# Four small loads moved out of a layer kernel's start, one normalisation a tick later, weight splits after attention steps

## The chip, the cores and the metric

The kernel runs on one core of one Trainium2 chip. The metric is device time in microseconds (us) of one execution; several runs are made and their median is quoted. Five engines matter here: PE (TensorE, matrix products), DVE (VectorE), ACT (ScalarE), POOL (GpSimd) and SP (SyncE, which here only issues transfers). POOL issues transfers as well. PEld is the load of the stationary operand of a product, which overlaps PE.

## The reference

One decoder layer on 512 tokens of width 1024. The input x is RMS-normalised and goes through one wide input projection. Three token mixers read it: block-sparse attention with partial rotary positions (MoBA, 8 heads of 64), forgetting attention with a cumulative log-gate bias (FoX, 8 heads of 64), and attention into 256 memory tokens (4 heads of 128). Queries and keys are normalised per head. The three results are projected, gated by sigmoids, summed and projected again; a SwiGLU feed-forward network follows. Cut to what the change touches:

```
h   = rms_norm(x, g_mix)
q_m = partial_rope(rms_norm(split_heads(q_m), g_q_moba))     # k_m alike
log_f = log_sigmoid(f_logit + b_forget)
mkv = rms_norm(mem, g_mem) @ w_mem_kv
y_c = softmax(q_c mk^T * scale) mv                           # memory attention
out = x + merged @ w_out, then + SwiGLU(rms_norm(.))
```

## The kernel before, in words

Every float32 product is made of three products: each operand is split into a rounded high half and the remainder (PASSES at L35: high by high, high by low, low by high). A weight arrives from HBM as a piece of 512 KB (`load_next`, L170, issued on SP), ACT writes its high half (`w_hi`, L234) and DVE subtracts to get the low half (`w_lo`, L237). `split_next` (L208) does one such piece; the low half of a piece is queued in `w_lows` and is issued by the next call, or by `take` (L252), which hands a finished piece to the products. Some pieces are sums of others (`w_sum`, L222), for a fast matrix product with seven instead of eight block products (`unit`, L764).

The order of all instructions is written out by hand. PE's products go through `mm` (L307), which counts their nominal time and calls `tick` (L291) every 1250 ns. A tick issues, in this order: what `head` holds, one weight split, what is due (`later(n, fn)`: n ticks from now, L328), steps of the work that runs beside (`beside`, L325: memory attention at 0.6 steps a tick, and so on), and what `pend` holds. A tick fixes only the order on each engine; when an instruction runs is settled by the semaphores. Each engine runs its list in order, so one that waits holds up all behind it.

The start goes like this. SP issues the two halves of the memory tokens, then weight pieces and the four tiles of x in turn (L408 to L423). POOL issues eight loads of small gains (L424 to L430), then four more: the rotary table of 64 KB (L432), two rows of 16 gains sent to all 128 partitions (L434, L435) and the eight forget biases sent to all partitions (L437). PE turns the memory tokens and multiplies them into memory keys and values (`mem_groups`, L521), 12 products to a piece. Beside it, one step a tick: two empty steps, `small_gains` (L482, which ends in six POOL products that make the rotary factors `cg` and `sg`, L494 and L497), the squares of x's four tiles (`square_x`, L656, on ACT), one empty step, squares of the memory, and then PE's turning of x (`turn_x`, L672, L676), two blocks a tick.

x's normalisation goes in two halves, `rms_x(0)` and `rms_x(1)` (L667). Each is three stages in `rsqrt` (L350): the variance on DVE (`rv`, L366), an estimate on ACT (L370, L371) and a Newton step on DVE (L374 to L376), and then `scale_x` (L660): POOL scales tiles 0 and 1, DVE scales tiles 2 and 3 (L663).

Then come the query projection of memory attention (`head_chunk`, L908; its 96 products make some 16 ticks), the gate parts, and two seven-product units, with memory attention beside them (`mem_attention`, L914). A step of it has, for one unit u of eight, scores on PE (L922), the row minimum on DVE (L930, L931), the exponentials on ACT (L939), the reciprocal on DVE and the scaling on POOL at the next tick (L943, L946), and three steps later PE's turning of the probabilities (L957), split by ACT and DVE (`memph`, `mempl`), and the values product (L968, split into `yT`). PE's results go to five banks of PSUM with the tag "a" and three with "m", in turn.

Of the kernel before, what the change touches and what calls it, by code (L numbers as in the profile page):

```python
# [17 lines left out]
P = 128  # L18
# [4 lines left out]
D = 1024  # L23
# [14 lines left out]
def f32(ap):  # L38
    return ap.bitcast(F32)
# [3 lines left out]
def hybrid_layer(ctx, tc, rope, x, mem, g_mix, w_in, b_forget, g_q_moba, g_k_moba, g_q_fox,  # L43
                 g_k_fox, g_q_mem, g_k_mem, g_mem, w_mem_kv, w_br_moba, w_br_fox, w_br_mem,
                 w_out, g_ffn, w_gate, w_up, w_down, out):
    nc = tc.nc
# [9 lines left out]
    def slot(name, dt=F32):  # L56
        return U.tile([P, SLOT], dt, name=name, tag="u", bufs=NSLOT)
# [26 lines left out]
    def dsrc(t, offset, pattern):  # L84
        return bass.AP(tensor=t.tensor, offset=t.offset + offset, ap=pattern)
# [72 lines left out]
    raws, split, used = {}, {}, {}  # L158
    st = {"load": 0, "split": 0, "take": 0, "stage": 0}
# [8 lines left out]
    w_lows = deque()  # L168
# [22 lines left out]
    def add_now(i):  # L191
        fn = accs.pop(i, None)
        if fn is not None:
            fn()

    def load_due():
        while st["load"] < len(loads):
            i = loads[st["load"]]
            if due.get(i, i - RAW_AHEAD) > st["split"]:
                return  # L200
            load_next()

    def drop(i):
        used[i] = used.get(i, 0) - 1
        if used[i] < 0:
            raws.pop(i)

    def split_next(least=0):  # L208


        if w_lows:
            w_lows.popleft()()
        i = st["split"]
        if i >= len(pieces) or i >= st["take"] + max(pace["ahead"], least):
            return
        kind, src, nk, w = pieces[i]
        n = nk * w
        if kind == "sum" and i not in raws:
            for j in src:
                add_now(j)  # L220
            r = raws[i] = slot("w_sum")
            dve.tensor_tensor(r[:, :n], raws[src[0]][:, :n], raws[src[1]][:, :n], op=OP.add)  # L222
            for j in src:
                drop(j)
            return
        add_now(i)
        if i not in split:
            split[i] = slot("w_hi", F32R), slot("w_lo", F32R)
        r, (hi, lo) = raws[i], split[i]
        if i < HALVES:  # L230
            c = slice(st["stage"] * n // 2, (st["stage"] + 1) * n // 2)
        else:
            c = slice(0, n)
        act.activation(hi[:, c], r[:, c], AF.Copy)  # L234

        def low():
            dve.tensor_tensor(lo[:, c], r[:, c], f32(hi[:, c]), op=OP.subtract)  # L237
        if i < HALVES:
            pend.append(low)
            st["stage"] = 1 - st["stage"]  # L240
            if st["stage"]:
                return
            run_pend()
            drop(i)
        else:
            w_lows.append(low)
            drop(i)
        split[i] = tuple(t[:, :n].rearrange("p (k c) -> p k c", k=nk) for t in (hi, lo))
        st["split"] += 1
        load_due()  # L250
# [13 lines left out]

    side = deque()
    deferred = []
    pace = {"credit": 0.0, "ns": 0, "ahead": 2}
    QUANTUM = 1250

    pend = []  # L270
# [1 line left out]
    def run_pend():  # L272
        for fn in pend:
            fn()
        pend.clear()
# [4 lines left out]
    def run_head():  # L280
        for fn in head:
            fn()
        head.clear()

    def run_due():
        due = [d for d in deferred if d[0] <= 1]
        deferred[:] = [[d[0] - 1, d[1]] for d in deferred if d[0] > 1]
        for d in due:
            d[1]()

    def tick():  # L291


        run_head()
        if w_lows or st["split"] < st["take"] + pace["ahead"]:
            split_next()
        run_due()
        if side:
            pace["credit"] += side[0][0]
            while pace["credit"] >= 1 and side:  # L300
                pace["credit"] -= 1
                side.popleft()[1]()
        if not side:
            pace["credit"] = 0.0
        run_pend()

    def mm(ps, lhsT, rhs, n, start, stop):  # L307
        if pace["ns"] >= QUANTUM:
            pace["ns"] = 0
            tick()  # L310
        pe.matmul(ps, lhsT, rhs, start=start, stop=stop)  # L311
        pace["ns"] += n * 0.42
# [12 lines left out]
    def beside(steps, rate):  # L325
        side.extend((rate, fn) for fn in steps)

    def later(n, fn):  # L328
        deferred.append([n, fn])
# [20 lines left out]
    def rsqrt(ss, inv_n, w, delay=None, rows=None, nh=1, out=None):  # L350

        v, y0, a, r = (sm(i, 32, 4 if i == "rr" else 3) for i in ("rv", "ry", "ra", "rr"))
        v, y0, a = v[:, :w], y0[:, :w], a[:, :w]
        r = r[:, :w] if out is None else out

        def by_rows(o, i):
            o3, i3 = (q.rearrange("p (t h) -> p t h", h=nh) for q in (o, i))
            dve.tensor_tensor(o3, i3, rows[:, :, None].to_broadcast([P, w // nh, nh]), op=OP.mult)  # L360

        def variance():
            if rows is not None:
                by_rows(ss, ss)
                by_rows(ss, ss)
            dve.tensor_scalar(v, ss, inv_n, EPS, op0=OP.mult, op1=OP.add)  # L366

        def estimate():
            use_table("natural_log_exp_and_others")
            act.activation(a, v, AF.Ln)  # L370
            act.activation(y0, a, AF.Exp, scale=-0.5)  # L371

        def newton():
            dve.tensor_tensor(a, y0, y0, op=OP.mult)  # L374
            dve.scalar_tensor_tensor(a, a, -0.5, v, op0=OP.mult, op1=OP.mult)
            dve.scalar_tensor_tensor(r, a, 1.5, y0, op0=OP.add, op1=OP.mult)  # L376
            if rows is not None:
                by_rows(r, r)
        for n, stage in enumerate((variance, estimate, newton)):
            if delay is None:  # L380
                stage()
            elif delay + n == 0:
                pend.append(stage)
            else:
                later(delay + n, stage)
        return r
# [42 lines left out]
    nc.gpsimd.dma_start(grow[GQC:GQC + 1], g_q_mem)  # L429
    nc.gpsimd.dma_start(grow[GKC:GKC + 1], g_k_mem)  # L430
    rope_t = first[:, 256:384].rearrange("p (t c) -> p t c", t=NT)
    nc.gpsimd.dma_start(rope_t, rope)  # L432
    grot = first[:, 384:416].rearrange("p (j c) -> p j c", j=2)
    nc.gpsimd.dma_start(grot[:, 0], dsrc(g_q_moba, 0, [[0, P], [1, 16]]))  # L434
    nc.gpsimd.dma_start(grot[:, 1], dsrc(g_k_moba, 0, [[0, P], [1, 16]]))  # L435
    bfor = consts.tile([P, 8], F32, name="bfor")
    nc.gpsimd.dma_start(bfor, dsrc(b_forget, 0, [[0, P], [1, 8]]))  # L437

    mz = consts.tile([P, 512], F32, name="mz")
    pool.memset(mz, 0.0)  # L440
# [41 lines left out]
    def small_gains():  # L482
        tg = bank("a")
        pe.transpose(tg[:, :NG], grow, ident[:NG, :NG])
        dve.tensor_copy(gcol, tg[:, :NG])
        for a in (0, 64):
            dve.memset(gcol[a:a + 16, GQM:GQM + 1], 1.0)
            dve.memset(gcol[a:a + 16, GKM:GKM + 1], 1.0)
        dve.tensor_scalar(gcol[:, GQF:GQM + 1], gcol[:, GQF:GQM + 1], -(64.0 ** -0.5), None, op0=OP.mult)
        dve.tensor_scalar(gcol[:, GQC:GQC + 1], gcol[:, GQC:GQC + 1], -(128.0 ** -0.5), None, op0=OP.mult)  # L490
        dve.tensor_scalar(gneg, gcol, -1.0, None, op0=OP.mult)
        for j in range(2):
            g = grot[:, j:j + 1, :].to_broadcast([P, NT, 16])
            pool.tensor_tensor(cg[:, j], rope_t[:, :, 0:16], g, op=OP.mult)  # L494
            for a in (0, 8):
                g8 = grot[:, j:j + 1, 8 - a:16 - a].to_broadcast([P, NT, 8])
                pool.tensor_tensor(sg[:, j, :, a:a + 8], rope_t[:, :, 16 + a:24 + a], g8, op=OP.mult)  # L497
# [156 lines left out]
    ssx = sm("ssx", NT, 1)  # L654
# [5 lines left out]
    def scale_x(t):  # L660
        r = rsx[t // 2][:, t % 2:t % 2 + 1]
        e = pool if t < 2 else dve
        e.tensor_scalar(x_t[t][:, :D], x_t[t][:, :D], r, 1.0, op0=OP.mult, op1=OP.mult)  # L663

    rsx = {}

    def rms_x(half):  # L667
        rsx[half] = rsqrt(ssx[:, 2 * half:2 * half + 2], 1.0 / D, 2, 0)
        later(2, lambda: scale_x(2 * half))
        later(2, lambda: scale_x(2 * half + 1))  # L670

    def turn_x(k, delay=None):  # L672

# [209 lines left out]
    def last_square(t):  # L883
        square_x(t)
        rms_x(t // 2)
# [17 lines left out]
    pre = None  # L903
    sums_of_h(6)
    pace["ahead"] = 3
    rs_q = consts.tile([P, NT * 4], F32, name="rs_q")
    nrs_q = consts.tile([P, NT * 4], F32, name="nrs_q")
    head_chunk(NT, 128, [(GQC, QC, h, gcol) for h in range(4)], lag=4, rs=rs_q)  # L908
# [254 lines left out]
        branch_part(bi, Y, jc)  # L1163


    later(9, lambda: beside(mem_attention(), 0.6))
    for jc in (0, 1):
        gate_part(0, jc)
# [1 line left out]
    tok_unit((heads_of("rope", GKM, KM, 0), heads_of("rope", GQM, QM, 0, gneg)))  # L1170
    tok_unit((values_of(VM, (0, 1)), values_of(VM, (2, 3))))
    pace["ahead"] = 2
    later(5, lambda: beside(attention((0, 1), QM, KM, VM, YM, None), 0.8))
    for jc in (0, 1):
        branch_part(0, YC, jc)
# [627 lines left out]
```

## Time and profile before

| | |
|---|---|
| median of 3 runs | 854.36 us (853.95 to 854.64) |
| the profiled execution, its own time | 853.07 us |
| its span, first to last instruction | 851.3 us, granted TensorE clock 1.00 |
| PE busy | 838.0 us (98%) |
| DVE, ACT, POOL busy | 688.5, 476.8, 202.1 us |

The time of the profiled execution is 1.8 us more than its span, and 1.3 us less than the median of the runs. Busy time on PE overlaps from one product to the next, so a gap that the profile shows is shorter than what was lost: the distance between two starts tells it.

### The profile page before, as it was taken

The numbers are of one execution on the slowest core, as the hardware profiler recorded it, in microseconds if no ns is written. First come the engines' busy times: TensorE is split into PE (matmuls) and PEld (weight loads), VectorE is DVE, ScalarE is ACT, GpSimd is POOL, SyncE is SP. The second block draws the span as 40 slices with busy tenths as digits, with TensorE's granted clock in tenths as the row PEclk, the third lists the DMA queues.
The fourth block names the chain that finished last, engine by engine and source line by source line (L and its number), as shares of the span: only waits on it lengthen the run. The fifth ranks groups of instructions, "written<-read, shape, count | busy, mean of one in ns | idle before, by whom it ended". The sixth has DMA issues, their size and how long they took to land.

```text
span 851.3 us, 14399 instructions
## 1 busy us (share of the span) xinstructions
PE 838.0 (98%) x5348; PEld 757.9 (89%) x5348; DVE 688.5 (81%) x1183; ACT 476.8 (56%) x820; POOL 202.1 (24%) x286
## 2 busy tenths in 40 slices
PE   7999999999999999999999999999999999999998
PEld 5778899899888889888999889999999999988886
DVE  4888799779686768877778757899989898897985
ACT  5946666576765648757435546453344444474571
POOL 5110428331532023324102021423210321110210
PEclk9999999999999999999999999999999999999999
DMA  9922357336922532754849546989955997864992
GB/s 308 352 37 75 75 134 188 51 100 184 290 74 59 165 76 80 175 92 142 255 128 287 204 129 128 228 174 209 178 132 112 183 183 179 215 151 149 245 250 91
DMA packets 146757, 137.66 MB, mean 162 GB/s; under 512 B 6192, under 2 KB 123496, under 8 KB 146688
## 3 DMA queue, kind: packets, MB, share of 16 engines
q1 hardware_dynamic: 111200, 104.65, 40.6%
q0 software_dynamic: 34304, 29.99, 23.1%
q10 hardware_dynamic: 1184, 2.12, 0.8%
q8 instruction: 42, 0.69, 0.3%
q14 instruction: 27, 0.22, 0.1%
HBM read 124.13 MB, written 8.40 MB: 156 GB/s over the span
## 4 chain that ended last, share of the span: by engine, by line
PE 87%; DVE 7%; ACT 3%; DMA 2%; issue 1%; SPq 0%; DVEq 0%; ACTq 0%
PE ps_m L311 38%; PE ps_a L1473 15%; PE ps_m L1473 11%; PE ps_a L1626 9%; PE ps_a L311 3%; PE ps_a L1062 3%; PE ps_a L1000 2%; PE ps_m L1626 2%; PE ps_a L1051 2%; DMA x_t<-in_x_dram 2%; DVE w_lo L237 2%; PE ps_a L606 1%; ACT p_t L939 1%; ACT w_hi L234 1%; PE ps_a L968 0%
## 5 line engine op out<-in xcount | busy, mean ns | idle before, releaser
L311 PE MATMUL ps_m<-w_hi,hT 128*128 128x256 f32 (+2 forms) x464 | 120.3, 335 | 0.0
L237 DVE TENSOR_TENSOR w_lo<-w_raw,w_hi 128x1024 fp32r<-128x1024 f32 (+2 forms) x90 | 105.0, 1180 | 7.9 <-ACT w_hi L234 7.0
L1473 PE MATMUL ps_a<-xh,wl 128*128 128x256 f32 x352 | 99.8, 284 | 0.1
L1473 PE MATMUL ps_a<-xh,wh 128*128 128x256 f32 x352 | 99.7, 283 | 0.0
L1473 PE MATMUL ps_a<-xl,wh 128*128 128x256 f32 x352 | 99.6, 283 | 0.0
L311 PE MATMUL ps_m<-hT,w_hi 128*128 128x512 f32 (+1 forms) x352 | 99.4, 369 | 0.0
L234 ACT ACTIVATE w_hi<-w_raw 128x1024 fp32r<-128x1024 f32 (+2 forms) x90 | 88.0, 1004 | 2.7 <-DMA w_raw<-in_w_in_dram 1.3
L311 PEld LDWEIGHTS ps_m<-w_hi,hT 128*128 128x128 f32 x464 | 80.1, 189 | 7.1
L1626 PE MATMUL ps_a<-dh,dr 128*128 128x512 f32 x242 | 76.5, 390 | 0.1
L311 PE MATMUL ps_m<-w_lo,hT 128*128 128x256 f32 (+2 forms) x232 | 76.0, 328 | 0.3 <-DVE w_lo L237 0.3
L1033 POOL TENSOR_SCALAR p_t<-p_t,rc 128x128 f32<-128x128 f32 (+1 forms) x64 | 46.0, 725 | 121.8 <-DVE rc L1032 70.7
L1473 PE MATMUL ps_m<-xh,wh 128*128 128x256 f32 x264 | 74.7, 283 | 0.0
L1473 PE MATMUL ps_m<-xl,wh 128*128 128x256 f32 x264 | 74.7, 283 | 0.0
L1473 PE MATMUL ps_m<-xh,wl 128*128 128x256 f32 x264 | 74.7, 283 | 0.0
L1307 POOL DMA_DIRECT2D wq<-in_w_gate_dram x22 | 32.9, 1494 | 164.5 <-DMA wq<-in_w_gate_dram 74.2
L1333 DVE TENSOR_TENSOR wl<-wq,wh 128x1024 fp32r<-128x1024 f32 x55 | 66.4, 1217 | 2.6 <-ACT wh L1330 2.6
L1473 PEld LDWEIGHTS ps_a<-xh,wl 128*128 128x128 f32 x352 | 67.6, 192 | 0.3 <-DVE wl L1333 0.3
L1473 PEld LDWEIGHTS ps_a<-xh,wh 128*128 128x128 f32 x352 | 67.6, 192 | 0.0
L1473 PEld LDWEIGHTS ps_a<-xl,wh 128*128 128x128 f32 x352 | 67.6, 192 | 0.0
L311 PEld LDWEIGHTS ps_m<-hT,w_hi 128*128 128x128 f32 x352 | 60.3, 190 | 7.7
L1516 ACT ACTIVATE z<-z 128x512 f32<-128x512 f32 x22 | 13.9, 632 | 90.8 <-DVE z L840 90.7
L1330 ACT ACTIVATE wh<-wq 128x1024 fp32r<-128x1024 f32 x55 | 55.6, 1048 | 14.7 <-PE ps_m L1473 9.7
(296 smaller groups left out, 2318.4 us busy)
## 6 DMA issues: line engine op xcount, KB each, us to landing
w_raw<-in_w_in_dram SPq DMA_DIRECT2D x47, 512.0 KB, 4.6
wq<-in_w_gate_dram SPq DMA_DIRECT2D x55, 256.0 KB, 5.5
wq<-in_w_up_dram SPq DMA_DIRECT2D x55, 256.0 KB, 5.8
dq<-in_w_down_dram SPq DMA_DIRECT2D x25, 512.0 KB, 5.7
wq<-in_w_gate_dram POOLq DMA_DIRECT2D x22, 256.0 KB, 7.5
wq<-in_w_up_dram POOLq DMA_DIRECT2D x22, 256.0 KB, 9.8
w_raw<-in_w_in_dram POOLq DMA_DIRECT2D x10, 512.0 KB, 6.3
dq<-in_w_down_dram POOLq DMA_DIRECT2D x10, 512.0 KB, 6.7
```

The costliest lines, as they stand in the source:

```text
L234: act.activation(hi[:, c], r[:, c], AF.Copy)
L237: dve.tensor_tensor(lo[:, c], r[:, c], f32(hi[:, c]), op=OP.subtract)
L311: pe.matmul(ps, lhsT, rhs, start=start, stop=stop)
L1000: pe.matmul(ps[:, :n], Q[p][:, s * 512 + i * P:s * 512 + (i + 1) * P], K[p][s][:, b * 512:b * 512 + n], start=b == 0, stop=b == 1)
L1033: pool.tensor_scalar(pt[:, :nk], pt[:, :nk], rc, 1.0, op0=OP.mult, op1=OP.mult)
L1051: pe.transpose(tb[:, j * P:(j + 1) * P], pt[:, j * P:(j + 1) * P], ident)
L1062: pe.matmul(yb[:, :256], V[p][:, j, 2 * s:2 * s + 2, :], PT[b][:, j, :], start=(j == 0 and b == 0), stop=(j == nj - 1 and b == 1))
L1307: e.dma_start(t[:, g * 512:(g + 1) * 512].rearrange("p (k c) -> p k c", k=4), dsrc(w, kh * 512 * DFF + f0 + fh * P, [[DFF, P], [P * DFF, 4 ...
L1330: act.activation(full(hi), full(r), AF.Copy)
L1333: dve.tensor_tensor(full(lo), full(r), f32(full(hi)), op=OP.subtract)
L1473: pe.matmul(ps[:, g * 256:(g + 1) * 256], w[a][:, g, k, :], r[b][:, k, :], start=n % 12 == 0, stop=n % 12 == 11)
L1626: pe.matmul(acc_d[m][t2], r[a][:, e * 256 + t2 * P:e * 256 + (t2 + 1) * P], w[b][:, e * 512:(e + 1) * 512], start=(p == 0 and e == 0 and ( ...
```

## The change

It has three parts. The four loads from L432 on go into a function `load_rope`, which runs 14 ticks after the memory products have ended, and the six POOL products into `rope_factors`, 30 ticks after it. In `rms_x` each stage of x's second half, and its scaling, comes one tick later. And between the point where memory attention is queued and five ticks after the second unit, a tick that finds work beside it issues the weight split after that work instead of ahead of it.

```diff
-    pace = {"credit": 0.0, "ns": 0, "ahead": 2}
+    pace = {"credit": 0.0, "ns": 0, "ahead": 2, "splits_behind": False}
...
         run_head()
-        if w_lows or st["split"] < st["take"] + pace["ahead"]:
-            split_next()
+        behind = bool(side) and pace["splits_behind"]
+        if not behind:
+            split_due()
         run_due()
         if side:
...
         if not side:
             pace["credit"] = 0.0
+        if behind:
+            split_due()
         run_pend()
+
+    def split_due():
+        if w_lows or st["split"] < st["take"] + pace["ahead"]:
+            split_next()
...
     rope_t = first[:, 256:384].rearrange("p (t c) -> p t c", t=NT)
-    nc.gpsimd.dma_start(rope_t, rope)
     grot = first[:, 384:416].rearrange("p (j c) -> p j c", j=2)
-    nc.gpsimd.dma_start(grot[:, 0], dsrc(g_q_moba, 0, [[0, P], [1, 16]]))
-    nc.gpsimd.dma_start(grot[:, 1], dsrc(g_k_moba, 0, [[0, P], [1, 16]]))
     bfor = consts.tile([P, 8], F32, name="bfor")
-    nc.gpsimd.dma_start(bfor, dsrc(b_forget, 0, [[0, P], [1, 8]]))
+
+    def load_rope():
+
+        nc.gpsimd.dma_start(rope_t, rope)
+        nc.gpsimd.dma_start(grot[:, 0], dsrc(g_q_moba, 0, [[0, P], [1, 16]]))
+        nc.gpsimd.dma_start(grot[:, 1], dsrc(g_k_moba, 0, [[0, P], [1, 16]]))
+        nc.gpsimd.dma_start(bfor, dsrc(b_forget, 0, [[0, P], [1, 8]]))
...
         dve.tensor_scalar(gneg, gcol, -1.0, None, op0=OP.mult)
+
+    def rope_factors():
         for j in range(2):
...
     def rms_x(half):
-        rsx[half] = rsqrt(ssx[:, 2 * half:2 * half + 2], 1.0 / D, 2, 0)
-        later(2, lambda: scale_x(2 * half))
-        later(2, lambda: scale_x(2 * half + 1))
+        rsx[half] = rsqrt(ssx[:, 2 * half:2 * half + 2], 1.0 / D, 2, half)
+        later(2 + half, lambda: scale_x(2 * half))
+        later(2 + half, lambda: scale_x(2 * half + 1))
...
     sums_of_h(6)
     pace["ahead"] = 3
+    later(14, load_rope)
+    later(30, rope_factors)
...
+    pace["splits_behind"] = True
     later(9, lambda: beside(mem_attention(), 0.6))
...
     pace["ahead"] = 2
+    later(5, lambda: pace.update(splits_behind=False))
     later(5, lambda: beside(attention((0, 1), QM, KM, VM, YM, None), 0.8))
```

## Rows read from the trace of the kernel before

**Rows 1.** The page: busy us (share) by engine; a group's count, busy us, mean ns.
```profile
PE 838.0 (98%) x5348; PEld 757.9 (89%) x5348; DVE 688.5 (81%) x1183; ACT 476.8 (56%) x820; POOL 202.1 (24%) x286
...
L234 ACT ACTIVATE w_hi<-w_raw 128x1024 fp32r<-128x1024 f32 (+2 forms) x90 | 88.0, 1004 | 2.7 <-DMA w_raw<-in_w_in_dram 1.3
```

**Rows 2.** Busy time by stretch: length, each engine (instructions), PEclk, DMA share, GB/s.
```profile
50.00:70.00 20.00, 20.00 (x97) 16.40 (x96) 15.24 (x29) 8.48 (x15) 2.80 (x2) 1.00 0.00 1
...
130.00:480.00 350.00, 349.78 (x2161) 312.73 (x2160) 277.02 (x623) 215.98 (x422) 97.18 (x177) 1.00 0.56 150
```

**Rows 3.** Timeline of PE, 22 to 32 us: start, us, instruction, [idle before <-releaser].
```profile
22.40 0.61 PE L311 MATMUL ps_m<-w_hi,mhT 128*128 128x512 f32 x2
24.36 0.50 PE L311 MATMUL ps_m<-w_lo,mhT 128*128 128x512 f32 x1 [1.34 <-DVE w_lo L237]
...
27.02 0.53 PE L676 MATMUL ps_a<-ident,x_t 128*128 128x128 f32 x2
...
29.56 0.50 PE L311 MATMUL ps_m<-w_lo,mhT 128*128 128x512 f32 x1
...
30.83 1.03 PE L676 MATMUL ps_a<-ident,x_t 128*128 128x128 f32 x8
31.62 0.48 PE L311 MATMUL ps_a<-w_hi,mhT 128*128 128x512 f32 x1
```

**Rows 4.** Timeline of DVE, 23 to 27 us.
```profile
23.00 0.17 DVE L366 TENSOR_SCALAR rv<-ssx 128x2 f32<-128x2 f32 x1 [3.19 <-ACT junk L658]
23.08 1.22 DVE L237 TENSOR_TENSOR w_lo<-w_raw,w_hi 128x1024 fp32r<-128x1024 f32 x1
...
25.06 1.01 DVE L376 SCALAR_TENSOR_TENSOR rr<-ra,ry 128x2 f32<-128x2 f32 x1
```

**Rows 5.** Timeline of ACT, 18 to 33 us.
```profile
18.47 1.06 ACT L658 ACTIVATE junk<-x_t 128x1024 f32<-128x1024 f32 x1 [1.48 <-DMA x_t<-in_x_dram]
...
31.47 1.26 ACT L339 ACTIVATE hT<-ps_a,gcol 128x512 fp32r<-128x512 f32 x2 [0.92 <-PE ps_a L676]
```

**Rows 6.** Transfers at 12.5 to 15 us, at 15 to 20 us, and the last small load.
```profile
DMA packets 210, 0.33 MB, mean 132 GB/s; under 512 B 57, under 2 KB 76, under 8 KB 210
...
q0 software_dynamic: 62, 0.01, 61.5%
...
DMA packets 656, 1.96 MB, mean 392 GB/s; under 512 B 71, under 2 KB 71, under 8 KB 656
...
bfor<-in_b_forget_dram POOLq DMA_DIRECT2D x1, 4.0 KB, 7.0
```

**Rows 7.** Single lines of the kernel: count, least/median/greatest ns, first to last start.
```profile
L663 DVE TENSOR_SCALAR x_t<-x_t,rr x2: 734/1175/1616, 26.1 to 27.6; 128x1024 f32<-128x1024 f32 x2
...
L494 POOL TENSOR_TENSOR cg<-first x2: 620/693/766, 13.6 to 15.5; 128x64 f32<-128x64 f32 x2
...
L497 POOL TENSOR_TENSOR sg<-first x4: 247/470/696, 14.2 to 16.5; 128x32 f32<-128x32 f32 x4
```

**Rows 8.** Timeline of POOL around the first steps of memory attention.
```profile
85.71 1.82 POOL L946 TENSOR_SCALAR p_t<-p_t,rc 128x256 f32<-128x256 f32 x2 [29.05 <-DVE rc L943]
...
91.67 0.93 POOL L946 TENSOR_SCALAR p_t<-p_t,rc 128x256 f32<-128x256 f32 x2 [1.60 <-DVE rc L943]
```

**Rows 9.** Timeline of DVE inside memory attention.
```profile
98.19 1.39 DVE L237 TENSOR_TENSOR w_lo<-w_sum,w_hi 128x1024 fp32r<-128x1024 f32 x1 [0.78 <-ACT w_hi L234]
99.50 1.21 DVE L222 TENSOR_TENSOR w_sum<-w_sum,w_raw 128x1024 f32<-128x1024 f32 x1
```

**Rows 10.** Timeline of PE inside memory attention.
```profile
95.77 0.60 PE L957 MATMUL ps_a<-ident,p_t 128*128 128x128 f32 x4
...
102.17 0.39 PE L311 MATMUL ps_a<-w_hi,xh 128*128 128x256 f32 x1 [0.39 <-DVE mempl L337]
...
105.05 0.63 PE L957 MATMUL ps_a<-ident,p_t 128*128 128x128 f32 x4 [0.47 <-DVE yT L337]
...
106.95 0.28 PE L311 MATMUL ps_m<-w_hi,xh 128*128 128x256 f32 x1
```

## The prediction

> **What bounds the kernel now.** I read the page first: PE is busy for 838.0 us of an 851.3 us span [rows 1], so only the 13 us in which it is not, and the little more that overlapping products hide, can be won by a change that removes no product. Busy time by stretch then tells where these are. From 130 to 480 us PE is busy for 349.78 of 350 us [rows 2]; what the change can win lies ahead of that, in the stretch that it touches, and since nothing behind waits for anything but PE, what PE gains there should reach the end whole.
>
> PE's timeline shows three losses near the start [rows 3]. Where nothing is late, five products of this shape stand between 29.56 and 30.83: 0.25 us each. The two at 22.40 are followed by one that starts at 24.36 instead of 22.90: 1.46 us lost, waiting for a weight's low half on DVE. The eight turnings of x that begin at 27.02 should take 0.79 us (30.83 to 31.62, where nothing waits); one product follows, and the next should start at 28.06. It starts at 29.56. That is 1.50 us more, spent first on the scaled x and then on the next low half. Together 2.96 us.
>
> DVE's timeline says why [rows 4]. It stood idle for 3.19 us until 23.00, because the variance of x's second half, next in its list, waited for ACT's square of the fourth tile. The low half that PE needed stood behind it and began at 23.08. So PE's loss hangs on ACT, and ACT's timeline shows that ACT itself was idle for 1.48 us until 18.47, waiting for x's second tile to land [rows 5]. The transfers show why that was late [rows 6]: from 12.5 to 15 us all engines together moved 0.33 MB, against 1.96 MB in the next 5 us. In that stretch 62 packets of POOL's queue, 0.01 MB in all, held the 16 engines for 61.5% of their time: 24.6 us for 62 packets, 0.40 us each. The load of the forget biases took 7.0 us for 4 KB.
>
> The last place is memory attention. PE waits 0.39 us until 102.17 and 0.47 us until 105.05, both times for a PSUM bank that DVE has yet to empty [rows 10]. Together 0.86 us, and a little more that the overlap of products hides.
>
> **The small loads.** At 392 GB/s the 2.5 us would have carried 0.98 MB; 0.65 MB were missing, which is 1.66 us [rows 6]. If the four loads are gone from there, x's second tile lands at about 16.8 us, before ACT is free at 16.99 (18.47 less 1.48), and ACT's whole list moves up by 1.48 us. Bounds: nothing, if the slow packets were a victim of something else; 1.66 us of transfer and so 1.48 us of ACT at most. I take the upper end, because the slow packets and the missing bytes are in the same 2.5 us, and the transfers run full again right behind it.
>
> The Trainium skill speaks against it: its page "DMA: Bandwidth & Descriptors", section "Why small descriptors are slow (HBM only)", gives a small packet a fixed overhead of a few cycles. By that, packets of POOL's queue would cost the others next to nothing, and the sum would hold only what the order gives, which is the first rival below. The row shows 0.40 us to a packet and not cycles, and the trace decides, but it does not show what made them slow.
>
> In its new place the step issues the same four transfers on POOL, past two of the accumulating weight loads that POOL issues. Tick 14 falls at about 59.7 us, and the stretch from 50 to 70 us has a DMA share of 0.00 [rows 2]; POOL has nothing to do in the 29.05 us until 85.71 [rows 8]. The factors are first read when the first unit's keys are turned by position, after the sixth of its products, so well behind 106.95 [rows 10]. I cost this at nothing; without that cover it would be the same 1.66 us, on weights that are not yet due.
>
> **The normalisation a tick later.** The variance now follows the low half that PE waits for. With the squares done 1.48 us earlier, at 21.5: ACT writes the next high half first (1.0 [rows 1], to 22.5), then the estimate (two small instructions, 0.4, to 22.9); DVE makes the low half (1.22 [rows 4], to 23.8), the Newton step (three small ones of 0.17, to 24.3) and the two scalings. One of these took 1616 ns while POOL scaled its own tiles and the other, alone, 734 ns [rows 7]; POOL's two tiles have their factors at about 20.9, some 3.4 us ahead of DVE's, so I take the shorter one twice and x is whole at 25.8. PE, without its stall of 1.46, comes to the turnings at 25.6 and needs the fourth tile at 25.9. All 2.96 us could go. But behind it ACT has no gaps: between 18 and 44 us its idle time is the 1.48 and, until 31.47, 0.92 us more [rows 5], and with both closed it is 2.40 us ahead, and PE with it. I take 2.4; bounds 0.9 (the first rival below) and 2.96.
>
> **Splits behind the attention steps.** In the tick around 98 us DVE first waits 0.78 us for a high half, subtracts (1.39) and adds (1.21) [rows 9], and only then finds the row minimum for which ACT's exponentials wait. Turned round, ACT works while DVE splits, DVE does not stand waiting for the high half, and the bank waits of 0.86 us shrink. Against it, high halves now queue behind exponentials on ACT. Bounds 0 and 0.86; I take 0.8, near the upper end, because the one wait of 0.78 that goes and the 1.21 of adding that moves behind the minimum are each longer than either bank wait.
>
> **The moved products.** Two of 0.693 us and four of 0.470 us [rows 7], 3.3 us of POOL, now at tick 30, about 85 us, between the scalings of the second and the third unit. The third unit is scaled by 92.60 and turned on PE at 95.77 [rows 8, 10]: 3.2 us of cover. Bounds 0 and 3.3 us, all of them on PE's path; I take 0, because of the cover (the second rival takes less of it for granted).
>
> **The sum.** 2.4 + 0.8 = 3.2 us. The profiled execution took 853.07 us, 1.8 of it outside the span; 849.9 would follow. It lies 1.3 us under the median of 854.36, so on the scale of the medians 851.2 us, 0.37% less. About 0.2% (1.7 us) is what a measurement of this kernel can tell from no change.
>
> **The rivals.** First, the small loads were not what held x back: the squares still end at 22.98. Then the estimate is done at 24.4, x is whole between 27.2 and 28.0 (scalings of 734 or 1120 ns), PE waits 1.3 to 2.1 us for it, and 0.9 to 1.7 us of the 2.96 are won; with the 0.8 that makes 852.3. For it speaks that so few bytes should do so much; against it the coincidence.
>
> Second, the moved products get in the way of attention. While POOL scaled x, a DVE instruction on two numbers took 1.01 us, against 0.17 for the variance [rows 4]. If each product holds DVE up by its own length, the third unit's reciprocal comes 3.3 us late, and its scaling takes the 1.82 us of the first unit instead of 0.93 [rows 8]: 4.2 us late against 3.2 of cover. PE loses 1.0 us, and the 0.8 is not won: 2.4 less 1.0, so 853.0. The Trainium skill has this as a rule, on the page "SBUF — State Buffer", section "SBUF: two separate sides": a port pair that the two engines share is locked for a whole instruction. The row of 1.01 us agrees. Against the rival stands that DVE has waits of its own there, in which such a hold costs nothing.
>
> Third, slower: low halves come too late for PE, being behind each step. The place is the two units from 92 us on, some nine pieces; the price is up to 1.2 us a piece, one subtraction. The low half begun at 98.19 ends at 99.58 and is used from 106.95 [rows 9, 10], so a piece must slip by 7.4 us, some five steps' worth of DVE work, before PE feels it. It decides from four pieces on (3.2 + 1.7 = 4.9 us); with five or six late, about 857.
>
> Last, nothing reaches the end, since DVE and ACT, nearly full from 36 to 44 us, give it all back: 854.4.
>
> **The chances.** The forecast 0.52, first rival 0.18, second 0.14, third 0.10, last 0.06. Faster by over 0.2% means under 852.65: all of the forecast, 0.10 of the first rival and 0.08 of the second, 0.70. Slower: the third, 0.10. The rest, 0.20, is within 0.2%. The range reaches from 850.0 (2.96 + 0.86 = 3.8, and half a microsecond for what overlap hides) to 853.9 (past the second rival by 0.9), which leaves out the third rival, the last and the tail of the second.
>
> **What would show it.** Right: POOL's queue empty and 380 to 400 GB/s at 13 to 15 us; ACT's second square at 17 us; DVE's variance of the second half behind a low half, with no wait near 3 us; PE going from memory products into the turnings without a gap; no bank wait at 100 to 105 us. Wrong: if the lull in the transfers stays without the loads, if it moves to 60 us with weights behind it, if PE waits at the third unit's turning, or if waits for low halves show up between 92 and 125 us.

## The result, and the profile after

The changed kernel takes 849.47 us (849.36 to 849.53, four runs) against 854.44 us (853.95 to 854.64, four runs): a ratio of 0.994, interval 0.9928 to 0.9952. That is 4.97 us less, and 0.53 us under the low end of the range given. The profiled execution of after took 849.36 us, 0.1 us under its median, with a span of 847.6 us; that of before had taken 853.07 us. From profile to profile 3.71 us were won, between the medians 4.97. The experiments are about that difference above all.

The page of after, PE's busy time and the shares of the chain that ended last (by engine):

```profile
PE 836.8 (99%) x5348; PEld 758.0 (89%) x5348; DVE 687.6 (81%) x1183; ACT 476.6 (56%) x820; POOL 200.5 (24%) x286
...
PE 93%; DVE 4%; ACT 3%; DMA 0%; issue 0%; DVEq 0%; ACTq 0%
```

Transfers of after at 12.5 to 15 us:

```profile
DMA packets 361, 1.01 MB, mean 403 GB/s; under 512 B 32, under 2 KB 32, under 8 KB 361
...
q1 hardware_dynamic: 361, 1.01, 104.2%
```

POOL's queue is gone from this stretch, and the rate is 403 GB/s where it was 132 [rows 6]. ACT's timeline of after shows what that does:

```profile
16.92 1.05 ACT L670 ACTIVATE junk<-x_t 128x1024 f32<-128x1024 f32 x1
...
21.32 1.04 ACT L234 ACTIVATE w_hi<-w_raw 128x1024 fp32r<-128x1024 f32 x1
```

The second square starts at 16.92 without a wait, where it started at 18.47 after a wait of 1.48 [rows 5]. DVE's timeline of after:

```profile
19.04 1.23 DVE L237 TENSOR_TENSOR w_lo<-w_raw,w_hi 128x1024 fp32r<-128x1024 f32 x1 [0.78 <-ACT w_hi L234]
...
21.45 0.61 DVE L373 TENSOR_SCALAR rv<-ssx 128x2 f32<-128x2 f32 x1 [0.72 <-ACT junk L670]
22.40 1.82 DVE L237 TENSOR_TENSOR w_lo<-w_raw,w_hi 128x1024 fp32r<-128x1024 f32 x1 [0.34 <-ACT w_hi L234]
```

The variance of x's second half stands behind the low half that PE needs, and waits 0.72 us instead of 3.19 [rows 4]. PE's timeline of after:

```profile
22.85 0.39 PE L318 MATMUL ps_m<-w_lo,mhT 128*128 128x512 f32 x1
...
25.34 0.50 PE L688 MATMUL ps_a<-ident,x_t 128*128 128x128 f32 x3
26.18 0.77 PE L688 MATMUL ps_a<-ident,x_t 128*128 128x128 f32 x5 [0.34 <-DVE x_t L675]
26.71 0.47 PE L318 MATMUL ps_m<-w_hi,mhT 128*128 128x512 f32 x1
27.02 0.39 PE L318 MATMUL ps_m<-w_lo,mhT 128*128 128x512 f32 x1
...
28.17 1.04 PE L688 MATMUL ps_a<-ident,x_t 128*128 128x128 f32 x8
```

The product that stood at 24.36 in before starts at 22.85, the one at 29.56 at 27.02 [rows 3]: 1.51 us are won by then, and 2.54 behind the turning. The next turnings start at 28.17 instead of 30.83, 2.66 us sooner, and PE stays that far ahead until memory attention, so the loads cost it nothing in their new place. One wait of 0.34 is left. In memory attention, busy time by stretch (PE, PEld, DVE, ACT, POOL, PEclk, DMA share, GB/s) has PE without a gap, and POOL's timeline shows where the moved products went:

```profile
100.00:110.00 10.00, 10.00 (x81) 9.63 (x80) 8.39 (x15) 7.93 (x16) 4.06 (x7) 1.00 0.06 13
```

```profile
87.49 0.93 POOL L960 TENSOR_SCALAR p_t<-p_t,rc 128x256 f32<-128x256 f32 x2 [2.19 <-DVE rc L957]
88.39 0.31 POOL L506 TENSOR_TENSOR cg<-first 128x64 f32<-128x64 f32 x1
...
89.37 0.45 POOL L509 TENSOR_TENSOR sg<-first 128x32 f32<-128x32 f32 x2
90.02 0.93 POOL L960 TENSOR_SCALAR p_t<-p_t,rc 128x256 f32<-128x256 f32 x2 [0.20 <-DVE rc L957]
```

Both bank waits of [rows 10] are gone. The product that started at 102.17 behind the first now starts at 99.04, and the one at 105.05 behind the second at 101.34: PE's lead grows from 2.67 to 3.13 and to 3.71 us, and it is 3.7 us in all that follows. The six moved products run from 88.39 to 89.82, 1.4 us in all, between two scalings, and the second of these still waits for DVE and not for POOL.

### The profile page after: what moved, and what is told of

It reads as the page before. It is cut to its first block, busy times and chain, and to the rows that moved or that the text cites. A ratio compares the mean times of both kernels' runs of the same rounds, so it can differ in the third digit from the quotient of the medians.

```text
span 847.6 us, 14411 instructions
## 1 busy us (share of the span) xinstructions
PE 836.8 (99%) x5348; PEld 758.0 (89%) x5348; DVE 687.6 (81%) x1183; ACT 476.6 (56%) x820; POOL 200.5 (24%) x286
## 4 chain that ended last, share of the span: by engine, by line
PE 93%; DVE 4%; ACT 3%; DMA 0%; issue 0%; DVEq 0%; ACTq 0%
PE ps_m L318 41%; PE ps_a L1489 15%; PE ps_m L1489 11%; PE ps_a L1642 9%; PE ps_a L318 3%; PE ps_a L1076 3%; PE ps_a L1014 2%; PE ps_m L1642 2%; PE ps_a L1065 2%; PE ps_a L618 1%; DVE w_lo L237 1%; ACT w_hi L234 1%; PE ps_a L936 1%; PE ps_a L982 1%; ACT junk L670 0%; DMA mem_h<-in_mem_dram 0%
```

## The experiments

The three parts of the change are called loads, norm (the normalisation a tick later) and splits here; the lull is the slow stretch of the transfers at 12.5 to 15 us.

**One quantity orders most of them**: the start S of ACT's second square, which is when x's second tile has landed and ACT is free. Each row below is one profiled execution; "line" is 851.6 + (S - 16.9), what e2 took and one microsecond more for each microsecond by which S is later.

```
kernel                           S      line    measured   less than the line
before                         18.47   853.17    853.07      0.10
e1  before once more           19.89   854.59    854.60      0.0
e2  loads                      16.90   851.60    851.60      -
e7  table of positions stays   17.13   851.83    851.76      0.07
e8  own addresses              17.02   851.72    851.62      0.10
e9  five loads                 19.94   854.64    854.67      0.0
e10 one load stays             18.27   852.97    853.00      0.0
e11 loads in SP's queue        19.10   853.80    854.13     -0.33
e13 seven loads, SP's queue    22.14   856.84    857.20     -0.36
e15 second tile loaded last    18.70   853.40    853.35      0.05
e4  splits                     19.05   853.75    852.60      1.15
e3  norm                       20.07   854.77    853.56      1.21
e12 norm once more             19.56   854.26    853.15      1.11
e5  loads and norm             17.15   851.85    850.66      1.19
e14 seven loads, norm          22.04   856.74    855.71      1.03
e16 second tile last, norm     18.67   853.37    853.82     -0.45
e6  norm and splits            19.60   854.30    852.12      2.18
after                          16.92   851.62    849.36      2.26
```

With norm and splits as in before, a microsecond of lateness of that tile is a microsecond of the kernel within 0.1 us, but for the two with loads in SP's queue, which lie 0.3 to 0.4 above the line. The norm and the splits are worth 1.0 to 1.2 us each in profiled executions, and they add up. e16 stands out; it comes last.

**e1, the kernel before once more**, no edit.

> The kernel before, unchanged, profiled once more. The profiled execution of before took 853.07 us and lay 1.3 us under the median of 854.4, while that of after lay on its median (849.36 against 849.47). Theory A, the lull in the transfers at 12.5 to 15 us differs in length from one execution to the next: executions spread over at least 0.7 us, and one that takes near 854.4 shows a lull longer than that of 853.07 by as much (x's second tile landing more than a microsecond later on ACT's timeline, or PE's stalls between 22 and 30 us summing to some 4 us and not 2.96). Theory B, the time differs in another part: the lull, ACT's wait for the second tile (1.48 us) and PE's stalls are the same, and the products behind 130 us lie further apart. Theory C, the profiled execution was an exception of its occasion: this profile too lies some 0.5 to 1.5 us under the median of its own runs, with the same rows.

Measured: 854.53 us (853.59 to 854.90, 11 runs), beside 29 other runs of before between 852.77 and 856.07; the profiled one took 854.60. ACT's timeline and the transfers at 12.5 to 15 us in it:

```profile
19.89 1.06 ACT L658 ACTIVATE junk<-x_t 128x1024 f32<-128x1024 f32 x1 [2.80 <-DMA x_t<-in_x_dram]
```

```profile
DMA packets 230, 0.41 MB, mean 165 GB/s; under 512 B 46, under 2 KB 68, under 8 KB 230
...
q0 software_dynamic: 55, 0.01, 56.5%
```

And PE's wait behind it:

```profile
25.78 0.50 PE L311 MATMUL ps_m<-w_lo,mhT 128*128 128x512 f32 x1 [2.68 <-DVE w_lo L237]
```

ACT's wait is 2.80 us instead of 1.48 [rows 5], and S is 1.42 us later in an execution that took 1.53 us more. PE's product stands at 25.78 instead of 24.36 [rows 3], 1.42 us later too, and from there to the end PE stays 1.4 to 1.5 us behind; the two waits in attention are the same (0.38 and 0.47). So theory A: the lull differs between executions, and the profile that the prediction rested on had caught a short one. Of the 123 measured executions of before, two took less than 853.1 us.

**e2, the loads alone** (with the products that read them):

```diff
-    nc.gpsimd.dma_start(rope_t, rope)
...
-    nc.gpsimd.dma_start(bfor, dsrc(b_forget, 0, [[0, P], [1, 8]]))
...
+    later(14, load_rope)
+    later(30, rope_factors)
```

> Only the loads (and the products that read them) are moved: POOL's queue is empty at 12.5 to 15 us; norm and splits as before. By the rows of the profiled execution x's second tile comes 1.48 us sooner and PE gains about 1.4 us. Theory A (the lull is longer in typical executions) adds its 1.3 us to the medians: 854.4 - 2.7 = 851.7, and the spread over executions shrinks to 0.2 us. Theories B and C: 853.0. The first rival of the prediction (the loads hold nothing up): 854.4.

Measured: 851.60 us, ratio 0.9972 (0.9961 to 0.9982), and all seven runs between 851.49 and 851.67. That is 2.8 us under before, theory A's number, and the spread of over 3 us has become 0.2. The forecast's first rival, that the loads hold nothing up, is ruled out.

**e3 and e12, the norm alone**, in two batches:

```diff
-        rsx[half] = rsqrt(ssx[:, 2 * half:2 * half + 2], 1.0 / D, 2, 0)
-        later(2, lambda: scale_x(2 * half))
...
+        rsx[half] = rsqrt(ssx[:, 2 * half:2 * half + 2], 1.0 / D, 2, half)
+        later(2 + half, lambda: scale_x(2 * half))
...
```

> Only the normalisation of x's second half is a tick later; loads and splits as before. DVE's variance stands behind the low half that PE waits for; the squares still end near 23.0 us. By the rows 0.9 to 1.7 us are won: 853.1 at the middle. Theory A: the spread of 0.7 us over executions stays, since the lull stays, and so does the profiled execution's distance from the median. If the order alone brings the whole 2.65 us that the start gained: 851.8.

> The norm alone once more, since its median (854.4) won nothing over before, though its profiled execution won 1.0 us at the same wait of ACT (wait 2.91, 853.56; the line of before gives 854.5 there), and on top of the loads it won 1.0 us in the median too. If its executions happened to have longer lulls that time: 853.4 now. If something in this kernel makes them longer, or PE pays more for a long one: 854.4 again, and where the profiled execution takes over 854.2, it shows either a wait of ACT above 3.5 us or more PE time behind the wait than ACT's wait explains.

Measured: 854.44 us (852.63 to 855.50), ratio 0.9999 (0.9990 to 1.0008), and 854.30 us (852.77 to 855.16), ratio 0.9997 (0.9988 to 1.0006): nothing in the median, where 853.1 was expected of e3, though both profiled executions lie 1.1 to 1.2 under the line. In e3's profile the stall has moved to the turning of x:

```profile
28.67 0.33 PE L676 MATMUL ps_a<-ident,x_t 128*128 128x128 f32 x1 [1.99 <-DVE x_t L663]
```

**e4, the splits alone** (the loads at their old place), **e5, loads and norm**, and **e6, norm and splits**. Their edits are those parts of the diff ahead of the prediction, the rest as in before; e4's core:

```diff
-        if w_lows or st["split"] < st["take"] + pace["ahead"]:
-            split_next()
+        behind = bool(side) and pace["splits_behind"]
+        if not behind:
+            split_due()
...
+        if behind:
+            split_due()
```

> Only the weight splits stand behind the steps beside the memory attention; loads and norm as before. By the two traces the attention gains 1.0 us: 853.4. Theory A: the spread of 0.7 us over executions stays. Theory B, where the 1.3 us lie in the part with the attention: 852.1. If the splits bring nothing by themselves and the 1.0 us come from the moved products or from the start: 854.4.

> The loads (with their products) and the norm, without the splits behind. The loads alone took 851.6 us and left PE a stall of two pieces at the turning of x and 0.3 us at the low half behind it; in after these were 0.34 us and nothing. If the parts add, the norm brings another 0.9 to 1.0 us on top of the loads: 850.6, with a spread under 0.3 us, and after lies 1.1 us below it, which is the attention's share. If the norm is worth nothing, as its median alone said (854.4): 851.6.

> The whole change without moving the loads. Theory A (the lull differs from one execution to the next, and every part that leaves it keeps its spread): spread over 1 us, median 852.1 to 853.1 (854.4 less 1.3 for the splits, less 0 to 1.0 for the norm). If the order alone brought the start's gain: 850.5 with a small spread.

Measured: e4 853.01 us (852.49 to 854.99), ratio 0.9988 (0.9979 to 0.9997); e5 850.60 us (850.38 to 850.80), ratio 0.9953 (0.9940 to 0.9965); e6 853.12 us (851.88 to 854.19), ratio 0.9985 (0.9976 to 0.9994). With e2 and after this gives the sum in medians: loads 2.8 (854.4 to 851.6), norm on top of them 1.0 (to 850.6), splits on top of both 1.1 (to 849.5). The expectations were 853.4 for e4, which took 0.4 less, and 852.1 to 853.1 for e6: it is at the upper end, and 0.1 above e4, so the norm wins nothing there either. e3, e4, e6 and e12, which keep the loads as they were, keep a spread of over 2 us.

**e7, only the three loads of equal bytes are moved**, the table of positions stays; **e8, own addresses**: everything stays, but each partition reads a row of x of its own.

```diff
# e7, against e2
+    nc.gpsimd.dma_start(rope_t, rope)
...
-        nc.gpsimd.dma_start(rope_t, rope)
# e8, against before
-    nc.gpsimd.dma_start(grot[:, 0], dsrc(g_q_moba, 0, [[0, P], [1, 16]]))
-    nc.gpsimd.dma_start(grot[:, 1], dsrc(g_k_moba, 0, [[0, P], [1, 16]]))
+    nc.gpsimd.dma_start(grot[:, 0], x[0, 0:P, 0:16])
+    nc.gpsimd.dma_start(grot[:, 1], x[0, P:2 * P, 0:16])
...
-    nc.gpsimd.dma_start(bfor, dsrc(b_forget, 0, [[0, P], [1, 8]]))
+    nc.gpsimd.dma_start(bfor, x[0, 2 * P:3 * P, 0:8])
```

> Only the three loads that give every partition the same 32 or 64 bytes are moved; the table of positions (128 packets of 512 bytes) stays in its place. If the lull is the work of the three: 851.6 as with all four moved, spread 0.2 us, x's second tile lands before ACT is free (no wait). If any packet of POOL's queue holds the engines up, in proportion to its number (128 of 512): about a quarter of the 2.8 us stays, 852.3. If it is the bytes (64 of 84 KB): nearly all stays, 853.8.

> The kernel before, with the three loads reading as many bytes in as many packets, but every partition its own address (a row of x each) instead of one address for all; the gains and biases are then other numbers. If the lull comes from 128 packets that read one address: it is gone, ACT's wait for x's second tile under 0.3 us, near 851.6. If it comes from small packets as such: waits of 1.5 to 3 us and 854.4 as before.

Measured: e7 851.67 us, ratio 0.9965 (0.9953 to 0.9978); e8 851.62 us, ratio 0.9965 (0.9952 to 0.9977), spread 0.26. In e8 nothing was moved in time. Its transfers at 12.5 to 15 us:

```profile
DMA packets 440, 0.91 MB, mean 362 GB/s; under 512 B 91, under 2 KB 123, under 8 KB 440
...
q0 software_dynamic: 96, 0.02, 5.3%
```

96 packets of POOL's queue held the engines for 5.3% of 16 times 2.5 us, 0.022 us each; in before 62 packets held them for 61.5%, 0.40 us each [rows 6]. These are means over unlike packets: by the trace's records of single packets 27 of the 62 and 48 of the 96 carry 4 bytes, and the others 512 or 256, eight of a load's 128 reads in each. Like against like, the three loads are 48 such packets in both kernels. They took 24.7 us in before, 0.51 each, 33.3 us in e1, 0.69 each, and 1.4 us in e8, 0.030 each. As many packets, as small, from the same queue, cost a seventeenth or less when each read has its own address.

So what made the lull is that 128 reads go to the same 32 or 64 bytes. e8 reads another tensor, too; but in before the same gains of q and k are also loaded for another use, and the eight packets of 256 bytes at 6.7 to 8.8 us, by size and number these two loads and two like them, took 0.018 us each. So it is not where these gains lie. The rule of the Trainium skill that the prediction weighed ("DMA: Bandwidth & Descriptors", section "Why small descriptors are slow (HBM only)": a small packet has a fixed overhead of some cycles) is not contradicted by e8's 0.030 us, and does not give before's 0.51. No run here shows what in the memory makes such reads slow.

**e9, five such loads; e10, one of the three stays** (against e2); **e11, the three in SP's queue**, behind the load of x's first tile:

```diff
# e9
+    again = consts.tile([P, 16], F32, name="again")
+    nc.gpsimd.dma_start(again[:, 0:8], dsrc(g_q_moba, 0, [[0, P], [1, 8]]))
+    nc.gpsimd.dma_start(again[:, 8:16], dsrc(g_k_moba, 0, [[0, P], [1, 8]]))
# e10
+    nc.gpsimd.dma_start(grot[:, 0], dsrc(g_q_moba, 0, [[0, P], [1, 16]]))
...
-        nc.gpsimd.dma_start(grot[:, 0], dsrc(g_q_moba, 0, [[0, P], [1, 16]]))
# e11
+    nc.sync.dma_start(grot[:, 0], dsrc(g_q_moba, 0, [[0, P], [1, 16]]))
+    nc.sync.dma_start(grot[:, 1], dsrc(g_k_moba, 0, [[0, P], [1, 16]]))
...
+    nc.sync.dma_start(bfor, dsrc(b_forget, 0, [[0, P], [1, 8]]))
     load_next()
...
-    nc.gpsimd.dma_start(bfor, dsrc(b_forget, 0, [[0, P], [1, 8]]))
```

> The kernel before with five loads that give every partition the same bytes instead of three: two more, of 32 bytes to a partition, into a tile that nothing reads. The profiles so far fit: time = 851.6 us and ACT's wait for x's second tile (1.48 gives 853.1, measured 853.07; 2.80 gives 854.4, measured 854.60). The median of 854.4 then stands for a wait of 2.8, or a lull of 3.0 with 0.2 us of cover: 1.0 us for a load. Theory A, a cost by packets on one address: five loads make a lull of 5.0, a wait of 4.8 and 856.4 us, with a wider spread. If the further loads come when the transfers have something else to wait for: 854.4.

> One of the three loads stays at its place (the gains of q, 128 packets of 64 bytes from one address), the other two and the table of positions are moved. At 1.0 us a load and 0.2 us of cover: a wait of 0.8, 852.4 us. If the lull needs several such loads at once: 851.6.

> The three loads that read one address are issued by SP, between x's first tile and what follows it, in the queue of the large loads, instead of POOL's queue. If the address makes the lull, whatever the queue: x's tiles behind them come 2 to 3 us late, 853.5 to 854.5 us, again with a spread. If POOL's queue is what makes such packets slow: 851.6 us, no wait of ACT beyond 0.3 us.

Measured: e9 854.77 us (853.54 to 856.14), ratio 1.0004 (0.9995 to 1.0013); e10 852.62 us (851.50 to 853.60), ratio 0.9980 (0.9972 to 0.9989); e11 854.80 us (853.70 to 856.31), ratio 1.0003 (0.9995 to 1.0012). One load costs 1.0 us over e2, where 0.8 was expected. Five were to cost 4.8 by theory A and cost 3.2, and ACT's wait in the profile, 2.79 us, is that of e1: theory A was wrong, and the time is near the other case's 854.4. The two further loads are last in POOL's queue, but that this is why they cost so little is not shown. In SP's queue the lull is much the same, and the time 0.3 above the expected range. Transfers of e11 at 12.5 to 15 us, with POOL's queue empty:

```profile
DMA packets 367, 0.28 MB, mean 112 GB/s; under 512 B 253, under 2 KB 253, under 8 KB 367
...
q1 hardware_dynamic: 367, 0.28, 33.7%
```

**e13 and e14, seven such loads in SP's queue**, in the order of before and with the norm a tick later (against e11; e14 has e3's edit as well):

```diff
+    again = consts.tile([P, 16], F32, name="again")
+    for a in (0, 4, 8, 12):
+        nc.sync.dma_start(again[:, a:a + 4], dsrc(g_q_moba, a, [[0, P], [1, 4]]))
```

> The order of before, with seven loads of one address each in SP's queue ahead of x's second tile (four more, of 16 bytes to a partition, into a tile that nothing reads), to make a stall of PE that is surely long. Three of them moved the start of ACT's second square from 16.9 to 19.1 us; seven move it to about 22.0. By the line that the profiles show (851.6 us for a start at 16.9, and as much more as it starts later) 856.7. Theory D (after a long stall PE's granted clock is at its lower level for a stretch, and products pay for it): the granted clock is under 1.00 in some stretch between 20 and 40 us and the time lies above the line, 857 to 859. Theory E (only the length of the lull counts): 1.00 throughout, on the line within 0.4 us.

> The same seven loads with the norm a tick later. By the line, less the 1.15 us that the norm won in profiled executions: 855.6. Theory D: it too shows a stretch at the lower clock, and here the products that run in it are on PE's path, so that the norm wins less than 1.15 us over the run with the seven alone, or nothing. Theory E (the norm's executions had longer lulls by chance or by their build): it wins 1.0 to 1.2 us.

Measured: e13 858.15 us (857.04 to 858.36), ratio 1.0043 (1.0030 to 1.0056); e14 856.05 us (854.65 to 857.49), ratio 1.0025 (1.0015 to 1.0036). S is 22.14, so in the profiles seven loads make the tile 5.2 us late where three in this queue make it 2.2 late: 0.75 each, in proportion. The medians are 6.5 and 3.2 above e2's, 0.9 and 1.1 each. A wait of PE in e13, and its busy time by stretch (PEclk, behind POOL, is the granted clock):

```profile
28.03 0.80 PE L311 MATMUL ps_m<-w_lo,mhT 128*128 128x512 f32 x1 [3.23 <-DVE w_lo L237]
...
20.00:25.00 5.00, 3.47 (x15) 2.30 (x13) 0.17 (x1) 2.83 (x6) 0.00 (x0) 1.00 1.03 404
25.00:30.00 5.00, 1.97 (x5) 1.59 (x6) 3.15 (x9) 4.73 (x13) 1.39 (x2) 0.55 1.05 387
30.00:35.00 5.00, 5.00 (x24) 4.09 (x23) 4.17 (x5) 3.87 (x9) 0.82 (x1) 0.77 1.07 369
```

PE's clock does fall around such a stall, to a mean of 0.55 between 25 and 30 us. But theory D's second half failed here: the norm wins 2.1 us between the medians, more than its 1.15.

**e15 and e16, the second tile loaded behind the third and the fourth**, e15 on e2, e16 on e5:

```diff
-        t = len(x_t)
+        t = (0, 2, 3, 1)[len(x_t)]
...
+    x_t.insert(1, x_t.pop())
```

> As e2 (only the loads moved), but x's second tile is loaded behind the third and the fourth: late by two transfers of 512 KB, 2.6 us at 400 GB/s, and late by the same in every execution. ACT's second square starts at about 19.4 us as in typical executions of before. By the line (851.6 us at 16.9) 854.1, spread under 0.4 us. If the lull costs in some other way than by this tile's lateness: near 851.6.

> As e5 (loads and norm), with the same late second tile. If the norm is worth 1.15 us whenever the tile is 2.5 us late, as the profiled executions said: 1.1 us under e15, 853.0. Theory D (behind such a stall PE's granted clock falls in most executions, and eats the norm's gain): within 0.4 us of e15, with a mean granted clock of 0.998 in its executions and stretches under 1.00 behind 25 us.

Measured: e15 853.25 us, all 12 runs between 852.93 and 853.43; ratio 0.9985 (0.9977 to 0.9994). e16 852.60 us (851.95 to 854.09), ratio 0.9980 (0.9971 to 0.9989). The tile came 1.8 us late and not 2.6, so the time is 0.85 under the expected one, and on the line. e16's runs fall into two groups: seven with a mean granted clock of 0.999 or 1.0 take 851.95 to 852.86, median 852.22, which is 1.0 less than e15; five with 0.997 or 0.998 take 853.70 to 854.09, which is 0.55 more than e15. All of e15's have 0.999 or 1.0. The profiled execution of e16 is one of the five:

```profile
25.00:30.00 5.00, 3.17 (x14) 2.42 (x13) 3.71 (x8) 4.89 (x12) 0.00 (x0) 0.82 1.08 365
30.00:35.00 5.00, 5.00 (x28) 4.18 (x28) 3.14 (x4) 3.12 (x6) 0.00 (x0) 0.84 1.10 349
```

Its PE timeline:

```profile
27.30 0.33 PE L689 MATMUL ps_a<-ident,x_t 128*128 128x128 f32 x1 [1.50 <-DVE x_t L676]
...
30.60 0.63 PE L318 MATMUL ps_m<-w_lo,mhT 128*128 128x512 f32 x1
31.02 0.63 PE L318 MATMUL ps_m<-w_hi,mhT 128*128 128x512 f32 x1
31.45 1.13 PE L689 MATMUL ps_a<-ident,x_t 128*128 128x128 f32 x8
```

and that of e15:

```profile
24.59 0.50 PE L318 MATMUL ps_m<-w_lo,mhT 128*128 128x512 f32 x1 [1.56 <-DVE w_lo L237]
...
28.02 0.33 PE L689 MATMUL ps_a<-ident,x_t 128*128 128x128 f32 x1 [0.22 <-DVE x_t L676]
...
30.61 0.39 PE L318 MATMUL ps_m<-w_lo,mhT 128*128 128x512 f32 x1
30.84 0.39 PE L318 MATMUL ps_m<-w_hi,mhT 128*128 128x512 f32 x1
31.07 1.04 PE L689 MATMUL ps_a<-ident,x_t 128*128 128x128 f32 x8
```

Behind the wait of 1.50 us the products of e16 stand 0.42 and 0.43 us apart, against 0.23 in e15: PE is at the lower of its two levels, 1.2 instead of 2.4 GHz, by the means of 0.82 and 0.84 from about 28.2 to 31.6 us. It comes to the turning 0.72 us ahead of e15 (27.30 against 28.02) and to the next 0.38 behind (31.45 against 31.07): the norm's gain goes in these four microseconds. The same split is in e3 and e12: 9 of their 22 runs, at 0.999 or 1.0, have a median of 853.15; the other 13, at 0.997 or 0.998, one of 854.66. In 123 runs of before the two groups lie only 0.4 apart (854.12 and 854.52). e6, with the norm, has three runs at 1.0 with a median of 852.04 and eight at 0.998 with 853.45; e4, without it, has groups 0.3 apart. By these groups the norm wins 1.0 us over before where the clock stays and nothing where it falls. That the falls are the reason is shown where the tile is late by the same in every run, e16 against e15. For e3, e6 and e12 it is argued: there the lull differs too, and no execution of theirs with a fall was profiled; in the profiles of e3 and e12 the clock stayed.

## Why the prediction was wrong

**The step that failed is the last one of the sum**: "It lies 1.3 us under the median of 854.36, so on the scale of the medians 851.2." It takes the distance between the profiled execution and the median, without a reason, for something that both kernels have. It was the lull's own: the profiled execution of before had a wait of 1.48 us for x's second tile, one at the median has some 2.8 (e1), and after has none, so it has no such distance (849.36 against 849.47). The loads were counted with the 1.48 us of one execution, a rare short one by bad luck, and are worth 2.8 us in the median (e2). Of the 1.73 us between 851.2 and 849.47 this step is 1.2. The range inherited it: its low end was the upper bounds taken from the median, without a longer lull.

**The rest of the miss, 0.5 us, is two terms sized too small.** The start was put at 2.4 and brought 2.66 from profile to profile (30.83 against 28.17). The cap of 2.40 came from ACT's idle times, of which the 0.92 in [rows 5] shrank to 0.51 in after, while two others ahead of it in the trace of before, 0.23 and 0.32 us, which the sum had left out, closed. With these the idle times that went come to 2.44 us; what makes up the rest is not in that list. The splits were put at 0.8 and brought 1.04, since the overlap of products hides part of what the two bank waits cost: 0.39 and 0.47 us in the view, 0.46 and 0.58 by the distances; e4's profile gives 1.15.

**The small loads** were rightly taken for the cause, against the Trainium skill's rule that the prediction weighed. The 0.40 us to a packet is a mean over unlike packets (0.51 for one that carries data), but e2, e7 and e8 show that the lull comes from them, from three of the four, and by their one address. **The normalisation** did as forecast, and with the loads gone it is worth 1.0 us in the median (e5). The first rival's case, the norm without the earlier tile, was put at 0.9 to 1.7 us; profiled executions gave 1.1 to 1.2, the medians nothing. The prediction did not think of the clock; that falls of it behind the wait left at the turning take the gain is shown for e16 and likely for e3 and e12.

**The moved products** cost nothing, as taken: they take 1.4 us instead of the 3.3 counted (0.31 us for one of those that took 0.693 [rows 7]). They run at 88.4 us and not at the 85 counted, but between the two scalings, as counted, and the third unit is scaled at 90.02, right behind them, when DVE's reciprocal is there. **The third rival**, late low halves, is ruled out by after's rows: between 92 and 125 us PE is busy for all of the 33 us and waits for no low half, and after is on the sum of its parts.

**Open** are three things: what in the memory makes reads of one address slow, and by a different amount in each execution; why in e16 PE's clock fell behind a stall of 1.50 us at 27 us in five runs of twelve, and in e15 never behind one of 1.56 us at 24 us, nor in the profiles of e1, e3 and e12 behind waits of 2.68, 1.99 and 2.00 us; and why e11 and e13 lie 0.3 to 0.4 us above the line.

## What to carry to other kernels

A load that gives all 128 partitions the same few bytes of HBM cost this kernel some 0.75 to 1.1 us, in either queue; it belongs where nothing is being loaded, as in after, or each partition should read an address of its own, as in e8. Where a stall hangs on transfers that collide, its length in one profile is one draw: compare the profiled execution with the median, and if it lies apart from it, ask first whether the part that you remove is what differs. And a change that only moves a stall can be worth nothing where PE's clock falls behind the new place, as in five of e16's runs, so look at the mean granted clock of every run, not only of the profiled one.

## What the runs showed of the hardware that was not expected

In POOL's queue a packet of eight reads of 32 or 64 bytes held an engine for 0.51 us in before, where all reads of a load go to one address, against 0.030 us in e8, with 128 addresses. In SP's queue each such read is a packet of its own, shown as 0.01 us in e11, and yet 367 packets moved at 112 GB/s there, with the engines busy for 33.7% of the time only. So a busy share does not always show such a lull; the rate does.

PE's granted clock fell to 1.2 GHz in the middle of an otherwise full kernel, behind a wait of 1.50 us (e16) and in one of 3.23 us (e13), and not behind others of up to 2.68 us. In e16 such a fall cost 1.6 us (853.80 against 852.22, the medians of its two groups). The Trainium skill's page "TensorE: Matmul & The Clock Gate", section "What's actually happening", has the clock set by how busy PE was lately; e13 and e16 agree in kind.
